# Hybrid encoder layer on one core: first modulation as matrix products, first loads reordered, and the first products of token half 0 placed ahead of the transposes of half 1

## Chip, core and metric

The kernel runs on one core of one Trainium2 chip. The metric is device time in microseconds (us) of one execution, the median of several runs. Engines are named as the profile names them: PE is TensorE (its weight loads are PEld), DVE is VectorE, ACT is ScalarE, POOL is GpSimd, SP is SyncE, whose queue here issues nearly all transfers.

## What is computed

One encoder layer over 1024 tokens of width 1024, all in float32. A conditioning vector gives shift and scale; the normalised, modulated input `h` goes through one wide projection `u = h @ w_in`, whose column groups feed four mixers.

```
cond = silu(c)
mod = cond @ mod_w + mod_b            # sh1, sc1, g1, sh2, sc2, g2
h = rms_norm(x) * (1 + sc1) + sh1
u = h @ w_in
y = concat(ssd(u), attention(u), mlstm(u), hyena(u)) @ w_out
x = x + g1 * y
h = rms_norm(x) * (1 + sc2) + sh2
x = x + g2 * ((silu(h @ w_gate) * (h @ w_up)) @ w_down)
out = rms_norm(x)
```

The Hyena mixer needs long filters that depend on weights alone: a small MLP of sines (`hyena_mlp`), a third product, a decay and a norm, then a 2048-point transform in two steps, sixteen-point sums on DVE and a table product on PE (`hyena_filters`). "First modulation" below is `sh1` and `sc1`, 2048 columns of `cond @ mod_w`.

## The kernel before

`build` (L286) runs the layer in one program. A scheduler reads the recorded operations and writes one fixed order of instructions for each engine; every engine then works through its own list in that order and waits where an operand is not ready. Tiles come from pools with a given number of buffers; a buffer that is taken again waits for its last reader.

The opening is `hyena_mlp` (L691), then `start` (L398) with `hyena_filters` (L717) interleaved, then the rest of `hyena_filters`, then `hyena` (L819).

- `start` loads the first modulation matrix as 16 pieces of 512 KB (`mw`, L416), four for each quarter q of the columns. For q of 0, 1 and 2 DVE multiplies each [128, 512] block by one column of `cond` and adds it to `acc` (L420, L422; eight blocks for each q); for q = 3 ACT multiplies (L425) and POOL adds (L427). PE transposes the four sums (L447), DVE reduces them over the 128 rows (L449) and adds the bias (L451, L452): `mod1`.
- The eight tiles `x` of 128 tokens are loaded (L435), ACT squares and sums them (L437), `norm` scales them (L442). For each token half h and each 128 columns k, PE transposes four blocks into one PSUM tile (L460, tile `tps`), ACT applies scale and shift (L462, `tm`), and `K.split` writes a high part (L235, `hhi`) and a low part (L239, `hlo`), the low part on POOL for even k and on DVE for odd k.
- Between the second and the third quarter of the modulation, `start` calls the first stage of `hyena_filters` (order 0): for each of eight blocks a product `fps` (L736), `hf` (L741), its square on ACT (L744), sums on DVE (L745, L749, L750) and a product with ones (L746).
- Between half 0 and half 1 it loads and splits the first weight group (`w_group`, L469).
- `hyena` then runs six columns groups of the projection: `gemm_t` (L483) is 24 products for each half of the tokens (three products of high and low parts for each of eight k, line L493), and `conv3` (L509) takes both halves out of PSUM.
- After the filters come the two convolutions (`hyena_conv`, L775). Their first product is L790 (`fps<-yk,tab`) and the first DVE operation on it is L798 (`ta<-fps,ks`).

PSUM is held in two pools of four tiles: `pg` for `tps`, `gps` and `nps`, `pm` for the rest.

Of the kernel before, what the change touches and what calls it, by code (L numbers as in the profile page):

```python
# [285 lines left out]
def build(nc, tc, d, out, dbg=None, dump=None):  # L286
    K = Net(nc, tc, d, out)
    with ExitStack() as es:
# [56 lines left out]
        with ExitStack() as e2:  # L345
            K.pm = psum("pm", right, m=4)
            hp = pool("ht", e2)
            K.so = Tags(pool("so", e2), st=3)
            with ExitStack() as e3:
                fl = Tags(rpool("fl", e3), n4=2, n2=8, yk=3, n1=2, tab=3, ks=3)  # L350
                hyena_mlp(K, fl)
                K.wp = Tags(pool("wp", e2), raw=3, whi=2, wlo=2)
                with ExitStack() as e4:
                    hf = hyena_filters(K, fl)
                    w0 = []
                    start(K, hp, Tags(pool("st", e4), tm=2), lambda: next(hf), lambda: w0.extend(w_group(K, G_HY + 2, first=False)))
                for _ in hf:
                    pass
            mp = Tags(rpool("m2", right), mxw=2)
            m2 = modulation2(K, mp)  # L360
            with ExitStack() as e3:
                hyena(K, Tags(rpool("hy", e3), n4=2, n2=8, yk=9, tab=3, tai=3, ks=2, rt=2), w0)
# [12 lines left out]
            mlstm(K, Tags(rpool("ml", right), va=2))  # L375
            project_na(K)
# [18 lines left out]
            _dump(K, dump)  # L395


def start(K, hp, sp, between, mid):  # L398

    nc, d = K.nc, K.d  # L400
    V = nc.vector

    accs, mts = {}, {}
    slots = [f"{t}{k}" for k in range(NK) for t in ("hhi", "hlo")]
    for qs in ((0, 3), (1,), (2,)):
        if qs == (2,):
            between()
        for q in qs:
            accs[q] = sp.tile([P, 512], F32, f"acc{q}")
        for k in range(NK):  # L410
            for q in qs:

                acc, c = accs[q], K.cond[:, k:k + 1]
                if k % 2 == 0:
                    mts[q] = hp.tile([P, 2, 512], F32, name="mw", tag=slots.pop(0))
                    nc.sync.dma_start(mts[q], d["modw1"][q, :, k:k + 2].rearrange("p k s c -> p k (s c)"))  # L416
                w = mts[q][:, k % 2]
                if q < 3:
                    if k == 0:
                        V.tensor_scalar_mul(acc, w, c)  # L420
                    else:
                        V.scalar_tensor_tensor(acc, in0=w, scalar=c, in1=acc, op0=ALU.mult, op1=ALU.add)  # L422
                else:
                    t = acc if k == 0 else sp.tile([P, 512], F32, "pr", bufs=2)
                    nc.scalar.activation(t, w, AF.Identity, scale=c)  # L425
                    if k > 0:
                        nc.gpsimd.tensor_tensor(acc, acc, t, op=ALU.add)  # L427
    ss = sp.tile([P, 8], F32, "ss")
    xs = []
    for g in range(4):  # L430
        xt = K.wp.tile([P, NK, 288], F32, ("whi", "wlo")[g % 2], name="x").rearrange("p a b -> p (a b)")
        for i in range(2):
            x = xt[:, i * D:(i + 1) * D]
            n = 2 * g + i
            nc.sync.dma_start(x, d["x"][n * P:(n + 1) * P, :])  # L435
            jk = K.so.tile([P, D], F32, "st", name="jk")
            nc.scalar.activation(jk, x, AF.Square, accum_out=ss[:, n:n + 1])  # L437
            xs.append(x)
# [5 lines left out]
    for q in (0, 3, 1, 2):  # L444
        ps = K.pm.tile([P, 512], F32, tag="m", name="psm")
        for n in range(4):
            nc.tensor.transpose(ps[:, n * P:(n + 1) * P], accs[q][:, n * P:(n + 1) * P], K.ident)  # L447
        mc = sp.tile([P, 2, 2], F32, "mc", bufs=2)
        V.tensor_reduce(mc, ps.rearrange("p (s k x) -> p s k x", s=2, k=2), axis=AX.X, op=ALU.add)  # L449
        mv = K.mod1.rearrange("p (s k) -> p s k", s=2)[:, :, 2 * q:2 * q + 2]  # L450
        V.tensor_tensor(mv, mc, K.pc[:, PC_MODB:PC_MODB + 16].rearrange("p (s k) -> p s k", s=2)[:, :, 2 * q:2 * q + 2], op=ALU.add)  # L451
        V.tensor_scalar_add(mv[:, 1], mv[:, 1], 1.0)  # L452
    K.hhi = [hp.tile([P, L], F32R, name=f"hhi{k}", tag=f"hhi{k}") for k in range(NK)]
    K.hlo = [hp.tile([P, L], F32R, name=f"hlo{k}", tag=f"hlo{k}") for k in range(NK)]
    for h in range(2):
        norm(h)
        for k in range(NK):
            ps = K.pg.tile([P, 512], F32, tag="g", name="tps")
            for i in range(4):
                nc.tensor.transpose(ps[:, i * P:(i + 1) * P], xs[h * 4 + i][:, k * P:(k + 1) * P], K.ident)  # L460
            t = sp.tile([P, 512], F32, tag="tm") if k % 2 else K.so.tile([P, 512], F32, "st", name="tm")
            nc.scalar.activation(t, ps, AF.Identity, bias=K.mod1[:, k:k + 1], scale=K.mod1[:, 8 + k:9 + k])  # L462
            c = slice(h * 512, (h + 1) * 512)
            K.split(K.hhi[k][:, c], K.hlo[k][:, c], t, "dve", "dve" if k % 2 else "pool")
        if h == 0:
            mid()


def w_group(K, n, gate=False, first=True):  # L469
# [10 lines left out]
    return whi, wlo  # L480


def gemm_t(K, whi, wlo, j):  # L483

    nc = K.nc
    c = slice(j * P, (j + 1) * P)
    pss = []
    for h in range(2):
        t = slice(h * 512, (h + 1) * 512)
        ps = K.pg.tile([P, 512], F32, tag="g", name="gps")  # L490
        seq = [(w, x, k) for k in range(NK) for w, x in ((whi, K.hhi), (whi, K.hlo), (wlo, K.hhi))]
        for n, (w, x, k) in enumerate(seq):
            nc.tensor.matmul(ps, lhsT=w[:, k, c], rhs=x[k][:, t], start=n == 0, stop=n == len(seq) - 1)  # L493
        pss.append(ps)
    return pss


def gemm_n(K, whi, wlo, i, N=256):
# [1287 lines left out]
```

## Time and profile before

| | |
|---|---|
| median of 3 runs | 1533.58 us (1527.52 to 1534.27) |
| the profiled execution | 1531.33 us, span 1529.5 us |
| PE busy | 1412.3 us, 92% of the span |
| DVE busy | 1043.3 us, 68% |
| ACT busy | 527.6 us, 34% |
| POOL busy | 91.4 us, 6% |
| mean granted TensorE clock | 0.974 of 2.4 GHz |
| HBM read and written | 195.17 and 60.59 MB |

Busy time is the time in which an engine had an instruction under way. The page cuts the span into 40 slices of 38.2 us; PE reads 2, 5, 8, 9 tenths in the first four, and 8 or 9 in nearly all later ones. DVE reads 7, 9, 9, 8, 9 in the first five. In the chain of work that ended last PE has 74% of the span, DVE 13%, DMA 5%.

### The profile page before, as it was taken

Reading aid. Unit: us, or ns where it says so; the run is one execution under the profiler, and the core shown is the slowest. Engines: PE = TensorE matmul, PEld = TensorE weight load, DVE = VectorE, ACT = ScalarE, POOL = GpSimd, SP = SyncE. Lnnn points to the kernel's source line nnn. Section 1 sums busy time; section 2 is a strip of 40 time slices with the busy share of each in tenths; the row PEclk is TensorE's granted clock in tenths of the full one; section 3 lists DMA queues with packets and bytes.
Section 4 is the critical chain, followed back from the end, with each engine's and each line's share of the span. In section 5 each row is a group of like instructions: output and inputs, shape, how many; then the busy total and the mean of one; then the engine's idle time right before and its main releaser. Section 6 shows DMA issues by size and latency. Waiting matters only on the chain.

```text
span 1529.5 us, 19231 instructions
## 1 busy us (share of the span) xinstructions
PE 1412.3 (92%) x6849; PEld 1141.0 (75%) x6849; DVE 1043.3 (68%) x2004; ACT 527.6 (34%) x958; POOL 91.4 (6%) x143
## 2 busy tenths in 40 slices
PE   2589979998998998989989999999999999999997
PEld 0366768876797777867767777888888888888886
DVE  7998977977847684687865476477777766335327
ACT  2522221232242342333456775322222223224222
POOL 2110000000102231230000000000000000000000
PEclk9789999999998999999999999999999999999999
DMA  6534467577653325476426457554444448643402
GB/s 247 194 104 143 128 197 230 185 225 226 190 185 110 105 87 155 125 265 203 154 87 217 150 170 276 201 180 164 148 144 153 149 164 305 222 149 123 153 1 110
DMA packets 134899, 257.02 MB, mean 168 GB/s; under 512 B 24703, under 2 KB 69663, under 8 KB 134804
## 3 DMA queue, kind: packets, MB, share of 16 engines
q1 hardware_dynamic: 111508, 228.50, 45.4%
q10 hardware_dynamic: 22688, 25.99, 4.8%
q0 software_dynamic: 608, 1.31, 0.3%
q8 instruction: 54, 0.88, 0.2%
q14 instruction: 41, 0.34, 0.1%
HBM read 195.17 MB, written 60.59 MB: 167 GB/s over the span
## 4 chain that ended last, share of the span: by engine, by line
PE 74%; DVE 13%; DMA 5%; issue 2%; ACT 2%; POOL 2%; SPq 0%; DVEq 0%; ACTq 0%; POOLq 0%
PE dps L1742 14%; PE X L1603 12%; PE gps L493 9%; PE Z L1603 8%; PE Y L1603 8%; PE gps L505 4%; PE gps L1554 3%; PE nS L1427 2%; PE ops L1554 1%; DMA mxw<-modw 1%; PE nS L1405 1%; DVE wlo L239 1%; PE kps L763 1%; PE mpa L1339 1%; DVE acc L422 1%
## 5 line engine op out<-in xcount | busy, mean ns | idle before, releaser
L1742 PE MATMUL dps<-wdh,ah 128*128 128x512 f32 x352 | 136.9, 389 | 0.0
L1742 PE MATMUL dps<-wdh,al 128*128 128x512 f32 x352 | 136.9, 389 | 0.0
L1742 PE MATMUL dps<-wdl,ah 128*128 128x512 f32 x352 | 136.9, 389 | 0.0
L493 PE MATMUL gps<-hhi,whi 128*128 128x512 f32 x320 | 130.7, 408 | 3.8 <-ACT nt L529 3.8
L493 PE MATMUL gps<-hlo,whi 128*128 128x512 f32 x320 | 129.6, 405 | 0.0
L493 PE MATMUL gps<-hhi,wlo 128*128 128x512 f32 x320 | 129.0, 403 | 0.0
L1603 PE MATMUL Z<-hp,wgh 128*128 128x512 f32 x352 | 95.4, 402 | 1.9 <-ACT ps L1658 1.6
L239 DVE TENSOR_TENSOR al<-ar,ah 128x1024 fp32r<-128x1024 f32 x44 | 53.4, 1222 | 47.9 <-ACT ah L233 47.9
L505 PE MATMUL gps<-whi,hhi 128*128 128x256 f32 (+1 forms) x256 | 77.5, 303 | 1.5 <-ACT z L529 1.5
L1603 PEld LDWEIGHTS Z<-hp,wgh 128*128 128x128 f32 x352 | 63.7, 188 | 19.8 <-ACT ps L1658 5.3
L505 PE MATMUL gps<-whi,hlo 128*128 128x256 f32 (+1 forms) x256 | 77.2, 302 | 0.0
L505 PE MATMUL gps<-wlo,hhi 128*128 128x256 f32 (+1 forms) x256 | 77.1, 301 | 0.0
L1742 PEld LDWEIGHTS dps<-wdl,ah 128*128 128x128 f32 x352 | 66.1, 188 | 13.8
L1742 PEld LDWEIGHTS dps<-wdh,al 128*128 128x128 f32 x352 | 66.1, 188 | 13.7
L1742 PEld LDWEIGHTS dps<-wdh,ah 128*128 128x128 f32 x352 | 66.1, 188 | 13.6
L493 PEld LDWEIGHTS gps<-hhi,whi 128*128 128x128 f32 x320 | 60.6, 189 | 19.5 <-ACT nt L529 5.0
L493 PEld LDWEIGHTS gps<-hhi,wlo 128*128 128x128 f32 x320 | 60.5, 189 | 13.8 <-issue 1.6
L233 ACT CAST ah<-ar 128x1024 fp32r<-128x1024 f32 x44 | 45.7, 1048 | 72.5 <-PE dps L1742 42.7
L493 PEld LDWEIGHTS gps<-hlo,whi 128*128 128x128 f32 x320 | 60.6, 189 | 12.4 <-issue 0.8
L1603 PE MATMUL X<-A,t4s 128*128 128x512 f32 x264 | 63.4, 389 | 0.0
L239 DVE TENSOR_TENSOR wdl<-wdr,wdh 128x1024 fp32r<-128x1024 f32 x22 | 26.9, 1224 | 53.1 <-ACT wdh L233 53.1
L1498 DVE SCALAR_TENSOR_TENSOR mxacc<-mxw,cond,mxacc 128x512 f32<-128x512 f32 x56 | 42.0, 750 | 29.2 <-DMA mxw<-modw 28.9
(500 smaller groups left out, 3240.5 us busy)
## 6 DMA issues: line engine op xcount, KB each, us to landing
wg<-wg SPq DMA_DIRECT2D x44, 512.0 KB
ar<-ad SPq DMA_DIRECT2D x44, 512.0 KB
mxw<-modw SPq DMA_DIRECT2D x64, 256.0 KB
raw<-w_in SPq DMA_DIRECT2D x28, 512.0 KB
psd<-ps SPq DMA_DIRECT2D x22, 512.0 KB
psr<-psd SPq DMA_DIRECT2D x22, 512.0 KB
wu<-wu SPq DMA_DIRECT2D x22, 512.0 KB
wdr<-wd SPq DMA_DIRECT2D x22, 512.0 KB
```

Source lines behind the costliest of these rows:

```text
L233: nc.scalar.copy(hi, src)
L239: e.tensor_tensor(lo, src, hi.bitcast(F32), op=ALU.subtract)
L422: V.scalar_tensor_tensor(acc, in0=w, scalar=c, in1=acc, op0=ALU.mult, op1=ALU.add)
L493: nc.tensor.matmul(ps, lhsT=w[:, k, c], rhs=x[k][:, t], start=n == 0, stop=n == len(seq) - 1)
L505: nc.tensor.matmul(ps, lhsT=x[k][:, t], rhs=w[:, k, :N], start=n == 0, stop=n == len(seq) - 1)
L763: nc.tensor.matmul(ps, lhsT=tab[:, la], rhs=y[:, 0], start=True, stop=not cx)
L1339: nc.tensor.matmul(pa[:, 2 * j + dr], lhsT=sds[dr][:, h], rhs=va[:, h], start=True, stop=True)
L1427: nc.tensor.matmul(pb[:, 448:512], lhsT=pT[:w * 40, n], rhs=vw[:w * 40, n, c:c + 64], start=n == 0, stop=n == len(chunks) - 1)
L1498: V.scalar_tensor_tensor(acc, in0=mt, scalar=K.cond[:, k:k + 1], in1=acc, op0=ALU.mult, op1=ALU.add)
L1554: K.nc.tensor.matmul(ps, lhsT=l, rhs=r, start=n == 0, stop=n == 5)
L1603: nc.tensor.matmul(ps, lhsT=w[a][:, k], rhs=x[k][b], start=start and n == 0, stop=n == 11, skip_group_check=not start)
L1742: nc.tensor.matmul(acc[i], lhsT=x[:, ts], rhs=m, start=f == 0 and n == 0, stop=f == NF - 1 and n == 2)
```

## The change

`start` becomes a generator that `build` drives in stages. The stages, in the order in which they are recorded: loads and squares of `x` tiles 0 to 3; `hyena_mlp`; loads of the modulation's quarter 0; load and split of the first weight group; loads of quarters 1 to 3 and of `x` tiles 4 to 7, then for each quarter its modulation and the two columns k of half 0 that need it; the products of the first weight group with half 0, both j (`gemm_half`); the columns of half 1; the products with half 1; and only then the first stage of `hyena_filters`.

The modulation of a quarter is eight float32 products on PE with one column of `cond` as the stationary operand (1 x 512 out), a copy of that row by ACT, four products that turn the row into four columns, and two small DVE operations. The sums on DVE, ACT and POOL and the reduction are gone. `x` tiles 0 to 3 have tiles of their own; the extra pool tag `tm` is gone, and all `tm` tiles come from the three `st` buffers.

```
+                    st = start(K, hp, Tags(pool("st", e4)))
+                    next(st)
+                    hyena_mlp(K, fl)
+                    next(st)
+                    w0 = w_group(K, G_HY + 2, first=False)
+                    next(st)
+                    pss = [[gemm_half(K, *w0, j, 0)] for j in range(2)]
+                    for _ in st:
+                        pass
+                    for j in range(2):
+                        pss[j].append(gemm_half(K, *w0, j, 1))
+                    next(hf)
...
+    for n in range(4):
+        load_x(n, sp.tile([P, D], F32, f"x{n}"))
+    yield
...
+    def load_w(q):
+        for k in range(0, NK, 2):
+            t = hp.tile([P, 2, 512], F32, name="mw", tag=f"{('hhi', 'hlo')[k // 2 % 2]}{2 * q + k // 4}")
+            nc.sync.dma_start(t, d["modw1"][q, :, k:k + 2].rearrange("p k s c -> p k (s c)"))
+            mts.append(t)
+
+    def modulation(q):
+
+        ps = K.pm.tile([P, 512], F32, tag="m", name="mps")[0:1]
+        for k in range(NK):
+            nc.tensor.matmul(ps, lhsT=K.cond[:, k:k + 1], rhs=mts[4 * q + k // 2][:, k % 2], start=k == 0, stop=k == NK - 1)
+        row = K.so.tile([1, 512], F32, "st", name="row")
+        nc.scalar.copy(row, ps)
+        mc = K.pm.tile([P, 512], F32, tag="m", name="mcs")[:, :4]
+        for i in range(4):
+            nc.tensor.matmul(mc[:, i:i + 1], lhsT=row[:, i * P:(i + 1) * P], rhs=K.ones[0:1, 0:1], start=True, stop=True)
...
+    load_w(0)
+    yield
+    for q in (1, 2, 3):
+        load_w(q)
+    xt = [K.wp.tile([P, NK, 288], F32, t, name="x").rearrange("p a b -> p (a b)") for t in ("whi", "wlo")]
+    for n in range(4):
+        load_x(4 + n, xt[n // 2][:, n % 2 * D:(n % 2 + 1) * D])
+    norm(0)
+    K.hhi, K.hlo = [], []
+    for q in range(4):
+        modulation(q)
+        for k in (2 * q, 2 * q + 1):
+            columns(0, k)
+    yield
+    norm(1)
+    for k in range(NK):
+        columns(1, k)
...
+def gemm_half(K, whi, wlo, j, h):
+
+    c = slice(j * P, (j + 1) * P)
+    t = slice(h * 512, (h + 1) * 512)
+    ps = K.pg.tile([P, 512], F32, tag="g", name="gps")
+    seq = [(w, x, k) for k in range(NK) for w, x in ((whi, K.hhi), (whi, K.hlo), (wlo, K.hhi))]
+    for n, (w, x, k) in enumerate(seq):
+        K.nc.tensor.matmul(ps, lhsT=w[:, k, c], rhs=x[k][:, t], start=n == 0, stop=n == len(seq) - 1)
+    return ps
```

`hyena` takes the two finished pairs of PSUM tiles instead of the weights. Lines after `start` move by 15: L736 becomes L751, L790 becomes L805, L798 becomes L813; the products L493 are L504, the transposes L460 are L458, L437 is L417.

What the scheduler makes of it shows at three places.

PE, where the first modulation ends and the transposes begin, before (`psm` are the transposes of the modulation's sums, `tps` those of `x`, `kps` table products of the filters, `gps` the first projection products):

```order
L447 MATMUL psm<-ident,acc_406 128x128 x4
L460 MATMUL tps<-ident,x 128x128 x48
L763 MATMUL kps<-yk,tab 128x256 x2
L460 MATMUL tps<-ident,x 128x128 x8
L763 MATMUL kps<-yk,tab 128x256
L460 MATMUL tps<-ident,x 128x128 x8
L765 MATMUL kps<-yk,tab 128x256
L493 MATMUL gps<-hhi_488,whi_590 128x512
```

and of the change, from the second product of the sine MLP to the third quarter of the modulation (`mps` is the row of a quarter, `mcs` its four columns, `x_200` to `x_212` the `x` tiles 0 to 3):

```order
L727 MATMUL fps<-h_226,w_220 64x512 x2
L436 MATMUL mps<-mw,cond 1x512 x8
L441 MATMUL mcs<-ones,row 128x1 x4
L436 MATMUL mps<-mw,cond 1x512 x8
L458 MATMUL tps<-ident,x_200 128x128
L458 MATMUL tps<-ident,x_204 128x128
L458 MATMUL tps<-ident,x_208 128x128
L458 MATMUL tps<-ident,x_212 128x128
L458 MATMUL tps<-ident,x_200 128x128
L458 MATMUL tps<-ident,x_204 128x128
L441 MATMUL mcs<-ones,row 128x1 x4
L436 MATMUL mps<-mw,cond 1x512 x8
```

The four quarters now stand on PE one behind the other, each behind the row copy of the quarter ahead of it, and the last two quarters and the 48 products of half 0 stand ahead of half 1.

ACT, of the change, around the copy of the first row (`h_237` is the output of the sine MLP, `jk,ss<-x` the squares of `x` tiles 4 to 7):

```order
L703 ACTIVATE h_237<-su 128x512
L417 ACTIVATE jk,ss<-x 128x1024 x4
L438 COPY row<-mps 1x512
L249 ACT_TABLE_LOAD
L249 ACTIVATE ln1t<-ln1v 128x4
L460 ACTIVATE tm<-tps,mod_66 128x512 x2
L438 COPY row<-mps 1x512
L460 ACTIVATE tm<-tps,mod_66 128x512 x2
```

The first row copy stands behind the squares of the last four `x` tiles, the last of the large loads of the opening.

DVE, before, from the end of the sine MLP into the filter loop (`acc_286`, `acc_406` are sums of the modulation, `hf`, `s`, `hp` and `hm` the filter loop):

```order
L687 TENSOR_SCALAR su<-su 128x512
L422 SCALAR_TENSOR_TENSOR acc_286<-mw,cond,acc_286 128x512 x5
L741 TENSOR_TENSOR hf<-fps,dc 128x512
L420 TENSOR_SCALAR acc_406<-mw,cond 128x512
L422 SCALAR_TENSOR_TENSOR acc_406<-mw,cond,acc_406 128x512
L745 TENSOR_TENSOR s_317<-s_317 128x256
L749 TENSOR_TENSOR hp<-hf 128x256
```

and of the change, from the last quarter's `mod` to the first filter operation:

```order
L443 TENSOR_TENSOR mod_66<-mcs,pc 128x2x2
L445 TENSOR_SCALAR mod_66<-mod_66 128x2
L235 CAST hhi_463<-tm 128x512
L235 CAST hhi_474<-tm 128x512
L239 TENSOR_TENSOR hlo_475<-tm,hhi_474 128x512
L235 CAST hhi_343<-tm 128x512
L756 TENSOR_TENSOR hf<-fps,dc 128x512
L235 CAST hhi_354<-tm 128x512
L239 TENSOR_TENSOR hlo_355<-tm,hhi_354 128x512
```

The filter loop has moved from ahead of the first `hhi` to behind the first `hhi` of half 1 (the second `hhi_343`, one and the same tile for both halves).

## Rows read from the trace of the kernel before

**Rows 1.** The page: busy time of each engine, share of the span, instructions.

```profile
PE 1412.3 (92%) x6849; PEld 1141.0 (75%) x6849; DVE 1043.3 (68%) x2004; ACT 527.6 (34%) x958; POOL 91.4 (6%) x143
```

**Rows 2.** Busy time by stretch: length, PE, PEld, DVE, ACT, POOL, clock, DMA share, GB/s.

```profile
82.25:219.52 137.27, 124.65 (x556) 96.97 (x555) 122.99 (x247) 39.71 (x60) 6.05 (x5) 0.96 0.43 134
0.00:82.25 82.25, 33.13 (x106) 17.02 (x107) 71.61 (x129) 33.02 (x54) 16.99 (x17) 0.84 0.64 218
```

**Rows 3.** Timeline of DVE: start, duration, line; first `hhi` of half 1, first convolution operation.

```profile
82.25 0.43 DVE L235 CAST hhi<-tm 128x512 fp32r<-128x512 f32 x1 [0.36 <-ACT tm L462]
...
219.52 0.69 DVE L798 TENSOR_TENSOR ta<-fps,ks 128x512 f32<-128x512 f32 x1 [1.22 <-PE fps L793]
```

**Rows 4.** Waits of DVE between 82.25 and 219.52: us in total, times, longest.

```profile
DVE ks L767 <- PE kps L765: 5.5, 6, 1.9
DVE n L551 <- ACT z L529: 2.5, 1, 2.5
```

**Rows 5.** Waits of PE between 86.04 and 219.52, same columns.

```profile
PE kps L763 <- DVE yk L591: 3.0, 1, 3.0
```

**Rows 6.** Groups of DVE by line, 0 to 82.25: busy, mean ns, idle before.

```profile
L422 DVE SCALAR_TENSOR_TENSOR acc<-mw,cond,acc 128x512 f32<-128x512 f32 x21 | 18.6, 885 | 0.4
...
L250 DVE RECIPROCAL fnr<-fnt 128x256 f32<-128x256 f32 x1 | 1.7, 1748 | 0.0
```

**Rows 7.** Timeline of DVE in the filter loop.

```profile
42.59 0.42 DVE L750 TENSOR_TENSOR hm<-hf 128x256 f32<-128x256 f32 x1
42.92 0.69 DVE L741 TENSOR_TENSOR hf<-fps,dc 128x512 f32<-128x512 f32 x1
43.52 0.42 DVE L745 TENSOR_TENSOR s<-s 128x256 f32<-128x256 f32 x1
```

**Rows 8.** Busy time of PE by stretch: length, PE, clock, DMA share, GB/s.

```profile
0.00:10.00 10.00, 1.97 (x4) 1.00 0.59 188
7.00:20.00 13.00, 2.42 (x6) 1.00 1.02 407
80.00:85.00 5.00, 4.99 (x23) 0.63 0.43 147
```

**Rows 9.** Timeline of SP's queue and ACT: first loads, a copy, a square, a `tm`.

```profile
2.12 0.43 SPq L695 DMA_DIRECT2D ft<-c_feats  x1
...
4.16 8.40 SPq L416 DMA_DIRECT2D mw<-modw  x12
...
19.95 1.18 ACT L713 COPY t<-fps 64x512 f32<-64x512 f32 x2 [0.83 <-PE fps L712]
...
40.90 1.06 ACT L437 ACTIVATE jk<-x 128x1024 f32<-128x1024 f32 x1 [0.76 <-DMA x<-x]
...
72.79 0.78 ACT L462 ACTIVATE tm<-tps,mod 128x512 f32<-128x512 f32 x1 [0.30 <-DVE hlo L239]
```

**Rows 10.** Timeline of PE: transposes after idle, first projection product, float32 products.

```profile
80.01 1.97 PE L460 MATMUL tps<-ident,x 128*128 128x128 f32 x8 [5.70 <-DVE x L442]
...
84.92 1.04 PE L460 MATMUL tps<-ident,x 128*128 128x128 f32 x8
...
86.04 0.58 PE L493 MATMUL gps<-hhi,whi 128*128 128x512 f32 x1
...
98.64 1.06 PE L765 MATMUL kps<-yk,tab 128*128 128x256 f32 x2
99.49 1.06 PE L763 MATMUL kps<-yk,tab 128*128 128x256 f32 x2
...
109.88 0.59 PE L763 MATMUL kps<-yk,tab 128*128 128x256 f32 x2
110.31 0.59 PE L765 MATMUL kps<-yk,tab 128*128 128x256 f32 x2
...
592.59 1.10 PE L1527 MATMUL mgp<-mxacc,ones 128*128 128x512 f32 x2 [0.81 <-DMA mxacc<-macc]
```

**Rows 11.** The chain that ended last, 100 to 112: start, us, what.

```profile
101.17 8.87 PE gps L493 x39
```

More of the change, by code (lines that the diff above doesn't have):

```diff
@@ L350, in build @@
                 fl = Tags(rpool("fl", e3), n4=2, n2=8, yk=3, n1=2, tab=3, ks=3)
-                hyena_mlp(K, fl)
                 K.wp = Tags(pool("wp", e2), raw=3, whi=2, wlo=2)
@@ L354, in build @@
                     hf = hyena_filters(K, fl)
-                    w0 = []
-                    start(K, hp, Tags(pool("st", e4), tm=2), lambda: next(hf), lambda: w0.extend(w_group(K, G_HY + 2, first=False)))
+                    st = start(K, hp, Tags(pool("st", e4)))
[10 more added lines that the diff above has]
+                    next(hf)
                 for _ in hf:
@@ L361, in build @@
             with ExitStack() as e3:
-                hyena(K, Tags(rpool("hy", e3), n4=2, n2=8, yk=9, tab=3, tai=3, ks=2, rt=2), w0)
+                hyena(K, Tags(rpool("hy", e3), n4=2, n2=8, yk=9, tab=3, tai=3, ks=2, rt=2), pss)
             project_ssd(K, lambda: next(m2, None))
@@ L395, in build, with start @@
             _dump(K, dump)
-def start(K, hp, sp, between, mid):
+def start(K, hp, sp):
     nc, d = K.nc, K.d
     V = nc.vector
[L403 to L427, printed above, removed]
@@ L428, in start, with load_x @@
     ss = sp.tile([P, 8], F32, "ss")
     xs = []
[L430 to L438, printed above, removed]
+    def load_x(n, x):
+        nc.sync.dma_start(x, d["x"][n * P:(n + 1) * P, :])
+        jk = K.so.tile([P, D], F32, "st", name="jk")
+        nc.scalar.activation(jk, x, AF.Square, accum_out=ss[:, n:n + 1])
+        xs.append(x)
@@ new lines, in start @@
+    for n in range(4):
+        load_x(n, sp.tile([P, D], F32, f"x{n}"))
+    yield
+    mts = []
+    def load_w(q):
[12 more added lines that the diff above has]
+            nc.tensor.matmul(mc[:, i:i + 1], lhsT=row[:, i * P:(i + 1) * P], rhs=K.ones[0:1, 0:1], start=True, stop=True)
+        mv = K.mod1.rearrange("p (s k) -> p s k", s=2)[:, :, 2 * q:2 * q + 2]
+        V.tensor_tensor(mv, mc.rearrange("p (s k) -> p s k", s=2),
+                        K.pc[:, PC_MODB:PC_MODB + 16].rearrange("p (s k) -> p s k", s=2)[:, :, 2 * q:2 * q + 2], op=ALU.add)
+        V.tensor_scalar_add(mv[:, 1], mv[:, 1], 1.0)
@@ L442, in norm @@
             V.tensor_scalar_mul(xs[4 * h + i], xs[4 * h + i], r[:, i:i + 1])
[L444 to L464, printed above, removed]
-        if h == 0:
-            mid()
+    def columns(h, k):
+        if h == 0:
+            K.hhi.append(hp.tile([P, L], F32R, name=f"hhi{k}", tag=f"hhi{k}"))
+            K.hlo.append(hp.tile([P, L], F32R, name=f"hlo{k}", tag=f"hlo{k}"))
+        ps = K.pg.tile([P, 512], F32, tag="g", name="tps")
+        for i in range(4):
+            nc.tensor.transpose(ps[:, i * P:(i + 1) * P], xs[h * 4 + i][:, k * P:(k + 1) * P], K.ident)
+        t = K.so.tile([P, 512], F32, "st", name="tm")
+        nc.scalar.activation(t, ps, AF.Identity, bias=K.mod1[:, k:k + 1], scale=K.mod1[:, 8 + k:9 + k])
+        c = slice(h * 512, (h + 1) * 512)
+        K.split(K.hhi[k][:, c], K.hlo[k][:, c], t, "dve", "dve" if k % 2 else "pool")
@@ L480, in w_group @@
     return whi, wlo
-def gemm_t(K, whi, wlo, j):
[L485 to L495, printed above, removed]
+def gemm_half(K, whi, wlo, j, h):
[6 more added lines that the diff above has]
+    return ps
+def gemm_t(K, whi, wlo, j):
+    return [gemm_half(K, whi, wlo, j, h) for h in range(2)]
 def gemm_n(K, whi, wlo, i, N=256):
@@ L816, in hyena_conv, with hyena @@
     dft16_inv(K, sp, g, Z)
-def hyena(K, sp, w0):
+def hyena(K, sp, pss0):
     nc = K.nc
@@ L824, in hyena @@
     for n in (1, 2, 0):
-        whi, wlo = w0 if n == 1 else w_group(K, G_HY + 2 * n)
+        w = n != 1 and w_group(K, G_HY + 2 * n)
         for j in range(2):
-            pss = gemm_t(K, whi, wlo, j)
+            pss = gemm_t(K, *w, j) if w else pss0[j]
             acc = K.so.tile([P, L], F32, "st", name="acc")
```

## Prediction

> **What bounds the kernel now.** I read the page first: PE is busy for 92% of the span, DVE for 68% [rows 1]. That is a mean over stages, so I looked for the point up to which the change reorders anything. Counting the instructions of both orders gives it: ahead of the first convolution product (`fps<-yk,tab`, L790) both kernels have done the same 288 projection products of line 493, the same 64 table products of the filters and the same 38 products of line 505, and DVE's list is the same again from its first operation on that product (`ta`, L798). I call this the common point; it stands at 219.52 us [rows 3]. Behind it both lists agree, so a delay there should be a delay of the whole kernel.
>
> Next I read busy time up to that point, cut at the first `hhi` of half 1 (82.25), which both kernels contain. From there to the common point DVE is busy 122.99 of 137.27 us and PE 124.65 [rows 2]. Both look full. The waits tell them apart: late in that stretch PE stands idle 3.0 us for a `yk` of the filters, a DVE result [rows 5], while DVE waits 5.5 us for products in six pieces and 2.5 once for ACT [rows 4]. So up to the common point the chain is DVE's list, with short trips through PE; PE is close behind. Ahead of 82.25 DVE is busy 71.61 of 82.25 us and PE only 33.13 [rows 2]. The opening is therefore DVE's, and the question is how much of DVE's work the new opening leaves for later.
>
> **What is removed.** 24 multiply-adds on DVE (21 take 18.6 us [rows 6]; the three first ones and the four reductions add some 4): about 22 us, and ACT's and POOL's quarter. This is the gain the change could have. It counts only if DVE does other work in that time.
>
> **The new opening, in order of time.**
>
> Loads. In the first 10 us 188 GB/s flow, 1.88 MB; saturated it is 407 GB/s [rows 8]. The first large load is now issued where `ft` was, at 2.12 and not at 4.16 [rows 9], so I count 1.88 MB at 8.0. Up to the last `x` tile 26 pieces of 0.524 MB and 0.31 MB of small ones must land: (13.94 - 1.88) / 0.407 = 29.6 us, so at 37.6.
>
> First row copy. Quarter 0 on PE is done by then, but the copy of its row stands on ACT behind the squares of `x` tiles 4 to 7, and each square takes 1.06 and a short read-out of its sum [rows 9]. The last ends near 38.9. The copy has one partition and 512 columns; the nearest row is 0.59 for 64 partitions [rows 9]. With four tiny products behind it quarter 1 starts on PE at 40.1.
>
> Quarters 1 to 3. No row shows a product with one column out. The price is that of the columns that stream: a float32 product over 256 columns follows the next after 0.43 at 2.4 GHz (109.88, 110.31) and after 0.85 at 1.2 GHz (98.64, 99.49) [rows 10], so over 512 it is 0.86 or 1.71. A quarter of eight is 6.9 at 2.4 GHz and 13.7 at 1.2. Alone, with other work between, one took 1.05 [rows 10], 8.4 for a quarter. Below nothing it can't cost, since PE has nothing else to do there. PE has idled before quarter 1. In the 5 us from 80, behind an idle stretch, the granted clock is 0.63 on average [rows 8], that is 3.7 us at 1.2 GHz and then 2.4, and eight transposes went from 1.97 at 80.01 to 1.04 at 84.92 [rows 10]. So quarter 1: 3.5 us at half speed for two products, six at 0.86, done at 48.8. Row copy and columns, partly under six transposes: 1.1. Quarter 2 done at 56.8, quarter 3 at 64.8, four transposes 0.5: the first products at 65.3, against 86.04 now [rows 10].
>
> Products of half 0. 48 at 8.87 / 39 = 0.227 [rows 11], 10.9 and 0.3 for the last columns: done at 76.5. The transposes of half 1 stand behind them. One group (0.5) and one `tm` (0.78 [rows 9]): DVE writes the first `hhi` of half 1 at 78.0. That is 4.2 us earlier than the 82.25 of now.
>
> DVE up to there. Scaling, two sine layers, two `wlo` and half 0 are some 22 us; DVE idles the other 56. The filter loop that filled this time stands behind the first `hhi` of half 1 in its list, so it can't start.
>
> DVE behind it. To the 122.99 us that it does today come eight rounds of the loop. From the starts, `hf` takes 0.60 and each of three others 0.33 [rows 7]: 8 x 1.59 = 12.7. Then the head of the transform that today lies ahead of 82.25: two operations over 1024 columns (1.2 each by the same pace), three over 512 or with a table (0.6), seven of 256 (0.33) and the reciprocal, 1.75 [rows 6]: 8.3 with the small ones, less what two finish under each other, 7.5. Together 20.2. So 143.2 us of DVE work. POOL's four low parts of half 1 run beside DVE in both kernels, so what they hold up is in the 123 already.
>
> Idle of DVE on the way: 14.28 now (137.27 - 122.99 [rows 2]). With PE now ahead of DVE, waits for queued products shrink, the dependent ends stay. Bounds 4 and 14; I take 8, since about half of the waits [rows 4] are such ends.
>
> **Sum.** 78.0 + 143.2 + 8 = 229.2 for the common point, against 219.5: **9.7 us later**. Against the profiled execution (1531.33) 1541.0; its time lies 2.25 under the median of the runs, 1533.58, so **1543.3** there. The lower end: quarters at full clock throughout (-2) and idle of 4 gives +4. The upper: 1.05 a product (+4.5) and idle of 14 gives +20. Other edits: the lost `tm` tag leaves three `st` buffers, hidden while DVE is the later engine; the 512 KB loads that leave the queue's later part are off the path; two free PSUM tiles of `pg` in the transposes of half 1 (two hold the products of half 0) slow them to ACT's 0.78 a column, still under DVE's pace of 1.2 or more.
>
> **Rivals.**
>
> *The clock stays at 1.2 GHz through the four quarters.* Quarters 1 to 3 then take 41.1 us and not 22.5, and the first 3.5 us of products run at half speed too: 18.6 + 1.8 = 20.4 more, so +30 (22 to 40), 1564. For it: a product with one column out is unlike anything in the trace. Against it: transposes, float32 table products and 64-row products all had the full clock once the work was dense. The Trainium skill ("TensorE: Matmul & The Clock Gate", section "What's actually happening") says that activity releases the throttle, and names no kind of product; for every kind that the trace holds it agrees. The same page ("Part 4: PE-mode transpose") says that transposes do not count as busy in the same way, by which kinds do differ; there the trace disagrees, since the transposes at 84.92 ran at full speed [rows 10].
>
> *Faster: PE sets the common point, not DVE.* PE reaches its first products 20.7 us earlier. Left over for later are 32 transposes (0.13 each [rows 10], 4.2), eight `fps` and eight sums (1.05 and 0.6 at most, halved where two `fps` run side by side: 9) and a few table products (2.2), 15.4, so PE is 5.3 us ahead; with the wait for `yk` [rows 5] gone as well, it is -8.3, about 1525. It decides whether DVE can write its last `yk` some 20 us sooner than I count, that is, whether the half 1 `hhi` comes at 60 and not at 78. The order speaks against it.
>
> *Absorbed: the delay is real at the common point and lost later*, because the convolutions wait for something that doesn't move. Price +0 to +4, 1535. Against it: every transfer of that stage is issued behind instructions that move with it.
>
> **How the numbers follow.** Forecast 0.55, half clock 0.25, absorbed 0.12, faster 0.08. A measurement of this kernel tells about 0.5% from no change, 7.7 us. Forecast at +4 to +20: a third of it lies under 7.7. So slower 0.25 + 0.37 + a little = 0.64, same 0.12 + 0.18 - a little = 0.28, faster 0.08. The range takes in the forecast's own +4 to +20, most of absorbed and all but the top of the half clock: 1533 to 1566; the forecast's own is 1537 to 1554.
>
> **What would show it.** Right: first products near 65; the first `hhi` of half 1 near 78; DVE idle for over 40 us before it; `ta` near 229; PE with many short waits for DVE from 90 to 220, where it now has few; behind `ta` the two traces run in step. The row copies' first one starts where the last square ends. Wrong: quarters of 13 us (half clock); `ta` at or ahead of 219 with DVE still full (DVE idles less than I think, or PE leads); a difference that grows or shrinks behind `ta`.

## Result and profile after

The changed kernel takes 1550.28 us (median of four runs, 1546.91 to 1554.95); the kernel before, run beside it, 1533.92. The ratio is 1.011 with a 95% interval of 1.0062 to 1.0159: **slower**, by 1.1%. The profiled executions are 17.2 us apart (1548.56 and 1531.33).

The busy row of the page and busy time by stretch, cut at the first `hhi` of half 1 and at the first `ta` (columns as in [rows 2]):

```profile
PE 1440.0 (93%) x6929; PEld 1143.7 (74%) x6929; DVE 1022.1 (66%) x1976; ACT 529.2 (34%) x956; POOL 79.5 (5%) x136
```

```profile
0.00:84.39 84.39, 60.00 (x194) 25.40 (x194) 28.90 (x57) 28.17 (x43) 5.50 (x9) 0.94 0.52 197
84.39:239.30 154.91, 126.73 (x548) 93.67 (x547) 142.79 (x292) 44.97 (x69) 6.07 (x6) 0.94 0.41 127
239.30:1546.70 1307.40, 1253.30 (x6191) 1024.60 (x6189) 850.42 (x1629) 456.08 (x845) 67.93 (x121) 0.99 0.51 169
```

DVE does 21 us less over the whole program (1043.3 before [rows 1]), PE 28 us more. Up to `ta` DVE's saving is 22.9 us: 28.90 + 142.79 = 171.7 against 71.61 + 122.99 = 194.6 [rows 2]. Yet `ta` comes 19.8 us later, since DVE's idle time ahead of the first `hhi` of half 1 went from 10.6 us to 84.39 - 28.90 = 55.5. Behind `ta` 1307.4 us remain, against 1529.5 - 219.52 = 1310.0 before: the delay is carried to the end, less 2.6 us.

The timeline of DVE at the two cuts (answers to [rows 3]), and DVE's waits between them (answers to [rows 4]):

```profile
84.39 0.43 DVE L235 CAST hhi<-tm 128x512 fp32r<-128x512 f32 x1 [8.04 <-ACT tm L460]
...
239.29 0.69 DVE L813 TENSOR_TENSOR ta<-fps,ks 128x512 f32<-128x512 f32 x1 [1.22 <-PE fps L808]
```

```profile
DVE ks L782 <- PE kps L780: 3.2, 7, 1.1
DVE n L566 <- ACT z L544: 2.5, 1, 2.5
DVE ks L782 <- DMA kspec<-ks: 2.2, 4, 1.0
DVE ta L813 <- PE fps L808: 1.2, 1, 1.2
```

The opening on ACT (the last square, the row copies of quarters 0 and 1) and on PE (the quarters, the first product, the last product of half 0, the first transposes of half 1):

```profile
39.45 1.06 ACT L417 ACTIVATE jk<-x 128x1024 f32<-128x1024 f32 x1 [0.64 <-DMA x<-x]
40.42 0.19 ACT L417 ACTIVATION_READ_ACCUMULATOR jk<-x 128x1 f32 x1
40.63 0.57 ACT L438 COPY row<-mps 1x512 f32<-1x512 f32 x1
...
52.98 0.57 ACT L438 COPY row<-mps 1x512 f32<-1x512 f32 x1 [7.85 <-PE mps L436]
```

```profile
24.23 8.98 PE L436 MATMUL mps<-mw,cond 128*1 128x512 f32 x16
41.35 1.83 PE L441 MATMUL mcs<-ones,row 1*128 1x1 f32 x8 [8.13 <-ACT row L438]
43.11 9.78 PE L436 MATMUL mps<-mw,cond 128*1 128x512 f32 x16
...
54.60 7.03 PE L436 MATMUL mps<-mw,cond 128*1 128x512 f32 x16
...
63.34 7.03 PE L436 MATMUL mps<-mw,cond 128*1 128x512 f32 x16
...
70.71 0.48 PE L504 MATMUL gps<-hhi,whi 128*128 128x512 f32 x1
71.12 1.05 PE L441 MATMUL mcs<-ones,row 1*128 1x1 f32 x8
...
82.65 0.39 PE L504 MATMUL gps<-hhi,wlo 128*128 128x512 f32 x1
82.88 1.03 PE L458 MATMUL tps<-ident,x 128*128 128x128 f32 x8
```

Quarter 0 is done at 33.2, and PE then waits 8.13 us for a row copy that stands behind four squares on ACT. From 43 to the last transposes of half 1 PE works without a gap, but what it works on is the modulation, and DVE waits for it. In the second stretch PE waits for DVE, longest of all for the last `yk` (at 208.9 and 226.0 us):

```profile
PE kps L778 <- DVE yk L606: 10.0, 2, 5.9
PE kps L778 <- DVE yk L563: 3.8, 3, 1.8
```

### The profile page after: what moved, and what is told of

Its sections match the earlier page's. It is cut to its first block, busy times and chain, and to the rows that moved or that the text cites. A ratio compares the mean times of both kernels' runs of the same rounds, so it can differ in the third digit from the quotient of the medians.

```text
span 1546.7 us, 19356 instructions
## 1 busy us (share of the span) xinstructions
PE 1440.0 (93%) x6929; PEld 1143.7 (74%) x6929; DVE 1022.1 (66%) x1976; ACT 529.2 (34%) x956; POOL 79.5 (5%) x136
## 3 DMA queue, kind: packets, MB, share of 16 engines
q1 hardware_dynamic: 111508, 228.50, 44.9%
## 4 chain that ended last, share of the span: by engine, by line
PE 75%; DVE 10%; DMA 7%; issue 3%; ACT 2%; POOL 2%; SPq 0%; POOLq 0%; DVEq 0%; ACTq 0%
PE dps L1757 14%; PE X L1618 12%; PE gps L504 10%; PE Z L1618 8%; PE Y L1618 8%; PE gps L520 3%; PE gps L1569 3%; PE nS L1442 2%; PE mps L436 2%; PE ops L1569 1%; PE nS L1420 1%; DMA mxw<-modw 1%; DMA x<-x 1%; PE mpa L1354 1%; DMA mkv<-mvk 1%
## 5 line engine op out<-in xcount | busy, mean ns | idle before, releaser
L504 PE MATMUL gps<-hhi,whi 128*128 128x512 f32 x320 | 130.9, 409 | 3.8 <-ACT nt L544 3.8
L504 PE MATMUL gps<-hhi,wlo 128*128 128x512 f32 x320 | 129.3, 404 | 0.0
L504 PE MATMUL gps<-hlo,whi 128*128 128x512 f32 x320 | 129.1, 403 | 0.0
L1757 PEld LDWEIGHTS dps<-wdh,al 128*128 128x128 f32 x352 | 66.1, 188 | 13.8
L504 PEld LDWEIGHTS gps<-hhi,whi 128*128 128x128 f32 x320 | 60.7, 190 | 19.6 <-ACT nt L544 4.9
L504 PEld LDWEIGHTS gps<-hhi,wlo 128*128 128x128 f32 x320 | 60.7, 190 | 13.9 <-issue 1.6
L504 PEld LDWEIGHTS gps<-hlo,whi 128*128 128x128 f32 x320 | 60.6, 189 | 12.4 <-issue 0.8
```

Source lines behind the costliest of these rows:

```text
L504: K.nc.tensor.matmul(ps, lhsT=w[:, k, c], rhs=x[k][:, t], start=n == 0, stop=n == len(seq) - 1)
L1757: nc.tensor.matmul(acc[i], lhsT=x[:, ts], rhs=m, start=f == 0 and n == 0, stop=f == NF - 1 and n == 2)
```

## Experiments

My theory going in: `ta` = first `hhi` of half 1 + DVE's work behind it + 12 to 16 us of waits. Rival: PE's work up to `ta` sets it. The table has all runs; its times are read from one profiled execution of each kernel. That the three terms add up to `ta` is so in any kernel; what the theory adds is that the waits stay between 12 and 16 us. "Idle ahead" is DVE's idle time before the first `hhi` of half 1. The ratio is that of all runs to the kernel before on the same chip; medians of different runs come from several chips, on which the kernel before took 1529.3 to 1533.9, so they are compared by their ratios.

| kernel | first `hhi` of half 1 | idle ahead | DVE work behind | waits behind | `ta` | ratio to before |
|---|---|---|---|---|---|---|
| before | 82.25 | 10.6 | 123.0 | 14.3 | 219.5 | 1 |
| changed | 84.39 | 55.5 | 142.8 | 12.1 | 239.3 | 1.0110 (1.0062 to 1.0159) |
| e1 loop between quarters | 101.58 | 50.8 | 120.6 | 15.4 | 237.5 | 1.0099 (1.0060 to 1.0139) |
| e2 half 1 first | 74.34 | 46.2 | 145.1 | 26.7 | 246.2 | 1.0142 (1.0100 to 1.0184) |
| e3 both | 88.80 | 48.9 | 130.9 | 23.0 | 242.7 | 1.0132 (1.0082 to 1.0183) |
| e4 squares late | 74.05 | 44.2 | 142.8 | 16.2 | 233.0 | 1.0084 (1.0049 to 1.0118) |
| e9 short quarters | 70.64 | 42.3 | 142.9 | 14.8 | 228.3 | 1.0062 (1.0038 to 1.0085) |
| e5 loop mid | 86.96 | 42.0 | 127.7 | 17.2 | 231.9 | 1.0064 (1.0040 to 1.0089) |
| e7 dense quarters | 83.58 | 40.3 | 129.3 | 14.9 | 227.8 | 1.0061 (1.0034 to 1.0087) |
| e8 quarter 0 first | 84.28 | 40.8 | 129.4 | 16.0 | 229.7 | 1.0065 (1.0048 to 1.0083) |
| e10 two quarters on PE | 82.29 | 17.7 | 119.8 | 13.3 | 215.4 | 0.9968 (0.9946 to 0.9990) |
| e11 all on PE | 88.18 | 33.5 | 117.8 | 13.3 | 219.3 | 1.0037 (1.0017 to 1.0058) |
| e14 half 0 ahead | 91.97 | 13.6 | 116.1 | 11.2 | 219.3 | 1.0016 (1.0000 to 1.0031) |
| e15 seven `dc` buffers | 85.03 | 16.7 | 116.9 | 16.7 | 218.6 | 0.9992 (0.9973 to 1.0011) |

The waits leave that range by more than 1.5 us in two rows, e2 and e3: there half 1 stands ahead of the products of half 0, and the rival was the better account.

### e1: the filter loop between the quarters (changed kernel)

```
-                    next(hf)
...
         modulation(q)
         for k in (2 * q, 2 * q + 1):
             columns(0, k)
+        filt()
...
-        if o == 0:
-            yield
+            if o == 0 and j in (4, 5, 6, 7):
+                yield
```

> Undoes one part of the change: the eight rounds of the filter loop are recorded two by two behind the four quarters of the modulation, not behind half 1. Theory (up to the common point the time is DVE's list, and the change left its opening idle and put 20.2 us of the filters behind the first hhi of half 1): DVE does the loop before that hhi, which itself moves by under 4 us; ta comes 12 to 20 us earlier than in the changed kernel (239.3), at 219 to 227, and the time falls by as much, to 1530 to 1538. Rival (PE's work up to the common point sets it): ta within 4 us of 239 and the time within 4 us of 1550. Second rival (squares and products of the loop between the quarters hold up ACT's row copies and PE): the first products come 5 us or more later than 70.7 and eat half of the gain or more.

Measured: median 1545.09; `ta` at 237.5. The second rival was right: the first products came at 83.33 and not at 70.71. DVE's work behind half 1 fell by 22 us, and the first `hhi` of half 1 came 17 us later. The timeline of PE, one quarter:

```profile
60.07 1.13 PE L751 MATMUL fps<-w,h 64*128 64x512 f32 x4
61.13 2.73 PE L435 MATMUL mps<-mw,cond 128*1 128x512 f32 x6
64.98 0.70 PE L761 MATMUL nps<-s,ones 128*128 128x256 f32 x2 [1.12 <-DVE s L760]
65.61 1.88 PE L435 MATMUL mps<-mw,cond 128*1 128x512 f32 x4
67.42 0.70 PE L761 MATMUL nps<-s,ones 128*128 128x256 f32 x2
68.04 2.74 PE L435 MATMUL mps<-mw,cond 128*1 128x512 f32 x6
...
72.50 1.13 PE L751 MATMUL fps<-w,h 64*128 64x512 f32 x4
```

The loop's products (1.06 and twice 0.63 by the starts) and one wait of 1.12 for a sum go into PE's series. A quarter's step is 12.4 us (72.50 - 60.07 from one `fps` to the next), not 8.74 (63.34 - 54.60). In an opening that PE sets, the loop is not free.

### e2 and e3: half 1 ahead of the products of half 0

```
-                    pss = [[gemm_half(K, *w0, j, 0)] for j in range(2)]
                     for _ in st:
                         pass
-                    for j in range(2):
-                        pss[j].append(gemm_half(K, *w0, j, 1))
+                    pss = [gemm_t(K, *w0, j) for j in range(2)]
```

e3 is e1 and e2 together.

> Undoes another part: both halves are transposed before any product of the first weight group; the loop stays behind half 1. Theory (DVE's list starts with the first hhi of half 1): that hhi no longer waits for the 48 products of half 0 and comes 11 to 12 us earlier, near 73; DVE's work behind it stays 143 us, so ta at 227 to 232 and the time 8 to 12 us shorter, 1538 to 1542. Rival (PE sets the common point): PE gives up 12 us of early products and waits for DVE's splits of half 1, so ta is the same or up to 6 us later, 1550 to 1556.

> Both edits together: loop between the quarters, and half 1 transposed ahead of the products of half 0. Theory: hhi of half 1 near 73 and 123 us of DVE work behind it with 8 to 14 us of waits would put ta at 204 to 212; PE, whose products of half 0 now come later, may then be the later one, so ta at 207 to 220 and 1520 to 1532; less than the sum of the two gains. Rival (PE sets the common point): no shorter than with the loop moved alone.

Measured: medians 1551.54 and 1550.67. In e2 the first `hhi` of half 1 came 10 us earlier, near where the theory had it, and `ta` 6.9 us later, by the rival's sign and a little beyond its 6. e3's `ta` is 5.2 us behind e1's: the rival there too. The waits of e2 say how; of DVE behind that `hhi`, and of ACT from it to 140 us:

```profile
DVE ks L780 <- PE kps L778: 9.2, 14, 1.3
DVE wlo L239 <- ACT whi L233: 8.3, 2, 8.1
...
ACT whi L233 <- PE gps L502: 9.6, 2, 5.2
```

PE starts the first products at 79.7, ACT stands with `acc` behind them, the next group's `whi` behind `acc`, and DVE's `wlo` behind that. So in this order the 48 early products, which hold the first `hhi` of half 1 back by 10 us, were worth more at `ta` than those 10 us. In the kernel before the same move (e14 below) is worth nothing.

### e4: squares of tiles 4 to 7 behind the row copies

```
         nc.sync.dma_start(x, d["x"][n * P:(n + 1) * P, :])
-        jk = K.so.tile([P, D], F32, "st", name="jk")
-        nc.scalar.activation(jk, x, AF.Square, accum_out=ss[:, n:n + 1])
         xs.append(x)
...
+    for n in range(4, 8):
+        square(n)
     yield
     norm(1)
```

> The squares of x tiles 4 to 7 are recorded behind the four quarters, so that the first row copy does not stand behind them on ACT. Nothing else moves. Theory (the opening is a chain, and the first row copy waits for a load that is not its own): quarter 1 starts near 35.6 and not at 43.1, the first products, the first hhi of half 1 and ta all come 6 to 8 us earlier, and the time is 1542 to 1544. Rival (the quarters wait for their matrix pieces, which land as late as the x tiles, or the squares only move the wait to half 1): first hhi of half 1 and time within 2 us of the changed kernel's 84.4 and 1550.

Measured: 1544.56, `ta` at 233.0 (6.3 us earlier). The first row copy on ACT and quarter 1 on PE:

```profile
32.07 0.57 ACT L442 COPY row<-mps 1x512 f32<-1x512 f32 x1 [1.82 <-PE mps L440]
```

```profile
33.74 7.03 PE L440 MATMUL mps<-mw,cond 128*1 128x512 f32 x16
```

Quarter 1 starts 9.4 us earlier than in the changed kernel and takes 7.03 us instead of 9.78: PE idles 0.8 us ahead of the columns and not 8.1, and the granted clock is 1.00 from 33.7 to 40.8 here, where it was 0.50 from 40 to 45 in the changed kernel. So the first products come 12.1 us earlier (58.60), 10.3 us of it arrive at the first `hhi` of half 1, and 4.1 of those are lost again to more waiting behind it.

### e9: the price of the quarters' products

```
-        for k in range(NK):
+        ks = range(NK) if q == 0 else (1, 7)
+        for k in ks:
```

> Prices the modulation on PE: quarters 1 to 3 keep two of their eight products (18 float32 products over 512 columns are left out, so most of the modulation of these quarters is missing); order, loads and everything else as in the changed kernel. Theory (the opening is PE's quarters in series, 7.03 us each, with row copy and columns between): first products 15 to 16 us earlier, near 55; first hhi of half 1 near 69 (84.4 now); ta 11 to 16 us earlier, 223 to 228; time 1534 to 1539. Rival (loads or ACT's row copies hold the opening): first products less than 8 us earlier, time over 1543.

Measured: 1537.99, first `hhi` of half 1 at 70.64, `ta` at 228.3. The 18 products at 0.88 (7.03 / 8) are 15.8 us; 14.3 arrive at the first products (56.38), 13.8 at that `hhi`, 11.0 at `ta`. By the ratios the gain is 0.5%, some 7 us, and their intervals overlap. This is the largest single piece of the loss that the runs show, 11.0 of the 19.8 us at `ta`.

### e5, e7, e8: what the opening gains without PE's gaps

All have the late squares of e4. e5 records the loop ahead of the products of half 0; e7 adds the next quarter's products ahead of this quarter's row copy; e8 adds the loads and products of quarter 0 ahead of `hyena_mlp`.

```
+                    next(hf)
                     pss = [[gemm_half(K, *w0, j, 0)] for j in range(2)]
...
+    products(0)
     for q in range(4):
+        if q < 3:
+            products(q + 1)
         modulation(q)
```

> On top of late squares (ta 233.0, first hhi of half 1 at 74.05, time 1544.6) the filter loop is recorded between the columns of half 0 and the products of half 0, so that it needs no PE between the quarters. Theory (the loop between quarters gained 19 us of DVE behind half 1 and lost 17 ahead of it, because PE waited for its sums): now DVE does the loop while PE does the products of half 0; first hhi of half 1 at 74 to 84, DVE's work behind it 123 to 130 us and not 143, ta at 214 to 226, time 1526 to 1537. Rival (PE has become the later engine up to the common point): ta at 229 or later and time over 1540.

> As the one before, and the eight products of the next quarter are recorded ahead of the row copy and columns of this one, so that PE has no gap between quarters (three gaps of 1.7 us in the changed kernel). Theory: first products 4 to 5 us earlier than with the loop alone, ta 2 to 5 us earlier, time 1522 to 1534. Rival (the matrix pieces land no sooner than PE asks for them): no difference.

> As the one before, and the loads and products of quarter 0 are recorded ahead of the sine MLP, so that PE does not hold them behind the MLP's product L727 (which starts at 22.3 in the changed kernel, quarter 0 at 24.2). Theory (the four quarters in series on PE set the opening, from the time the first one starts): quarter 0 starts at 12 to 16, first products near 50, ta 4 to 9 us earlier than without, 206 to 218, time 1517 to 1528, under before's 1530. Rival (quarter 3 waits for its pieces, which land near 34, or the clock is low that early, so each product takes twice as long): first products and time within 3 us of the kernel without this edit.

Measured: 1539.61, 1539.75 and 1539.35; `ta` at 231.9, 227.8 and 229.7. All three lie above the range the theory gave, by 3, 6 and 11 us. e7's `ta` came 4.1 us earlier than e5's as expected, but its first products only 1.2 us earlier (57.14, 4 to 5 expected), and the median gained nothing. The loop left DVE's stretch behind half 1 (15 us less than e4), but it now lies with the products of half 0 ahead of half 1, whose first `hhi` came 13 us later. In e8 quarter 0 began at 12.1, but quarter 1 still ended at 39.1 (38.6 in e7):

```profile
12.10 8.95 PE L440 MATMUL mps<-mw,cond 128*1 128x512 f32 x16 [12.10 <-DMA mw<-modw]
20.98 1.08 PE L733 MATMUL fps<-ft,w 33*64 33x512 f32 x4
...
29.20 1.97 PE L741 MATMUL fps<-h,w 64*64 64x512 f32 x4 [5.25 <-ACT h L717]
31.10 7.99 PE L440 MATMUL mps<-mw,cond 128*1 128x512 f32 x16
```

Quarter 1 stands behind the sine MLP's second product in PE's list and waits for it as before; and the MLP's first product now stands behind quarter 0, at 20.98 (11.68 in e7), so that its second one comes 7 us later than in e7 (29.20, 22.05). DVE's idle time ahead of half 1 stays near 41 us in all three: in this order DVE has little to do while PE does the modulation.

### e10, e11: the modulation on PE in the order before

From the kernel before; loads, loop and halves stay as they are. e10 moves quarters 1 and 2, e11 all four.

```
+                if q in ON_PE:
+                    nc.tensor.matmul(acc, lhsT=c, rhs=w, start=k == 0, stop=k == NK - 1)
+                    if k == NK - 1:
+                        columns(q, acc)
-                if q < 3:
+                elif q < 3:
```

> The kernel before, with quarters 1 and 2 of the modulation on PE (eight products, row copy by ACT, four column products) and quarters 0 and 3 on DVE, ACT and POOL as before; loads, filter loop and order of the halves as before. Theory (ta comes 123 us of DVE work and 12 to 16 us of waits behind the first hhi of half 1, wherever that stands; before, DVE is full up to it and PE idle): 11 to 13 us of DVE sums go, PE's 14 us of products lie in its idle time, the first hhi of half 1 comes at 69 to 74 (82.25), ta at 206 to 213 (219.5), time 1517 to 1525 against before's 1530. Rival (PE in its own order has to wait for the loop's sums between the products, as when the loop stood between the quarters, or the last x tile holds the opening): that hhi at 80 or later, time within 4 us of before.

> The kernel before, with all four quarters on PE and nothing else of the change: loads, filter loop and order of the halves as before. Theory (the modulation on PE is a gain as long as the loop fills DVE beside it; what lost in the changed kernel is the order around it): 22 us of DVE work go from the opening, first hhi of half 1 at 64 to 76, ta at 201 to 215, time 1512 to 1527. Rival (four quarters in series on PE with the loop's products between them set the opening, whatever else): first hhi of half 1 at 82 or later, time 1530 or more.

Measured: e10 1524.70, which is **faster than both kernels** (by 0.3% against before, 1529.32 beside it), at the slow end of the theory's range; e11 1535.85, the rival. In both the first `hhi` of half 1 stood where the rival had it, and e10's `ta` lies behind the theory's 213: its time is in the range, its mechanism is not the theory's. e10's gain is 4.2 us at `ta` where 10 us of DVE work went (184.4 up to `ta`, 194.6 before); by the table it comes from 3.2 us less work and 1.0 less waiting behind that `hhi`, not from an earlier `hhi`. In e11 22 us of work went and 23 us of idle time came. The profiled execution of e11 (1530.87) is among its shorter ones, that of e10 (1530.18) among its longer ones, so e11's row in the table looks better than its median and e10's looks worse. The timeline of ACT in e11 (row copy of the last quarter, first and last square):

```profile
53.88 0.57 ACT L410 COPY row<-mps 1x512 f32<-1x512 f32 x1 [1.81 <-PE mps L439]
...
54.89 1.04 ACT L461 ACTIVATE jk<-x 128x1024 f32<-128x1024 f32 x1
...
62.16 1.04 ACT L461 ACTIVATE jk<-x 128x1024 f32<-128x1024 f32 x1
```

### e14: only the products of half 0 ahead

```
+                    def mid():
+                        w0.extend(w_group(K, G_HY + 2, first=False))
+                        pss.extend([gemm_half(K, *w0, j, 0)] for j in range(2))
```

> The kernel before, with only the 48 products of half 0 placed ahead of the transposes of half 1. Theory (in the changed kernel PE was the later engine without this, so it gained 7 us at ta there; in the kernel before DVE's list sets ta): the first hhi of half 1 moves from 82.25 to 84 to 93, DVE fills part of that with its next transform work, ta unchanged or up to 6 us later, time 1530 to 1536. Rival (it helps PE here as well): ta 4 to 8 us earlier, time 1522 to 1526.

Measured: 1531.50, `ta` at 219.3, the first `hhi` of half 1 9.7 us later: DVE did transform work in that time (78.4 us ahead of it, 71.6 before). As the theory had it, and a part of the change that by itself costs at most 0.3%.

### e15: e10 with seven buffers for `dc`

```
-fl = Tags(rpool("fl", e3), n4=2, n2=8, yk=3, n1=2, tab=3, ks=3)
+fl = Tags(rpool("fl", e3), n4=2, n2=8, yk=3, n1=7, tab=3, ks=3)
```

> The kernel with quarters 1 and 2 on PE, and seven buffers in place of two for the tiles dc of the filter loop. The loads of x stand behind those of dc in SP's list, and each dc load waits until the loop has read an older one: before and with two quarters on PE the x tiles were issued one by one from 34 to 46 us, with 145 GB/s from 30 to 40. Theory (that wait of SP, not DVE, held the first hhi when DVE had less to do, so that hhi stayed at 69 and the first of half 1 at 82): x tiles issued by 30, landed by 42, first hhi of half 1 at 72 to 78, ta at 205 to 212 (215.4), time 1514 to 1521 against before's 1529. Rival (PE's mixed list of loop and quarters sets the opening): x tiles earlier, but half 1 at 80 or later and the time within 3 us of 1524.7.

Measured: 1530.16, `ta` at 218.6. The theory fell, and half 1 stands where the rival had it, but the time is 5.5 us above e10's median (0.24% by the ratios, whose intervals overlap), outside the rival's 3 us too. By the table the first `hhi` of half 1 came 2.7 us later than in e10 and DVE waited 3.4 us more behind it; why stays open. SP issued all eight tiles in one go, where e10 issued four of them one by one from 34.15 and was done at 46.2; and ACT did not look at them until its row copy was done (SP's queue; ACT's row copy, first and last square):

```profile
34.30 6.10 SPq L459 DMA_DIRECT2D x<-x  x8
...
53.62 0.57 ACT L410 COPY row<-mps 1x512 f32<-1x512 f32 x1 [1.67 <-PE mps L439]
54.11 1.05 ACT L461 ACTIVATE jk<-x 128x1024 f32<-128x1024 f32 x1
...
61.39 1.04 ACT L461 ACTIVATE jk<-x 128x1024 f32<-128x1024 f32 x1
```

In the changed kernel the row copy waits behind squares whose tiles come late; here eight squares wait behind a row copy whose quarter comes late (in e10 at 50.47). Both are one list of ACT with the later item in front. That a kernel with squares ahead of the last row copy would turn e10's remaining idle time into a gain was read from these rows and not tried.

## Why the prediction was right, and what it missed

The sign, the mechanism and the range held; the size was 1.011, where 1543.3 / 1533.58 = 1.0063 was named. On the profiled executions I had 9.7 us and 17.2 came, near the upper end of the forecast's own +4 to +20. By my own steps:

- **The common point and what lies behind it** held. In all fourteen kernels `ta` lies between 215.4 and 246.2, and 1303.8 to 1313.0 us remain behind it: 1310.2 on average in the five with `ta` under 220, 1306.9 in the nine above 227. So most of a delay at `ta` stays, and a few us of it may come back (single executions); "absorbed later" fell as the account of this change.
- **Last `x` tile, first row copy**: the copy does start where the last square ends, at 40.63 instead of 38.9, and with its columns (1.83 at the low clock, where I had allowed 1.2 for both) quarter 1 began 3.0 us late.
- **Quarters**: 9.78 and twice 7.03 measured, 8.7 and twice 6.9 predicted. The price of a one-column product, taken from the columns that stream, was right. (The upper bound of 1.05 a product misread [rows 10], whose line says 1.10; by it the upper end lies some 1 us higher.) Quarter 1's slow part was too short in my sum: low clock for 3.5 us, where the rows below give it until 48.7 (0.63 on average from 45 to 50), that is 5.6 us of the quarter, and 9.78 - 7.03 = 2.75 us of loss where I had 1.8. The gaps were 1.71 and not 1.1. First products 70.7, not 65.3.
- **Products of half 0** took 12.3 us instead of 11.2, since quarter 3's column products (1.05) stand among them. The first `hhi` of half 1: 84.39, not 78.0. That is 6.4 of the 7.5 us that the sum missed: a chain of steps of which nearly all were a little longer than costed.
- **DVE behind it**: 142.8 us measured, 143.2 predicted. Idle of DVE: 12.1, where I took 8 between bounds of 4 and 14. That term was mis-sized by 4.1: I had PE's lead shorten the waits by 6; they went from 14.3 to 12.1, those for `kps` from 5.5 [rows 4] to 3.2. Behind `ta` 2.6 came back: 6.4 - 0.4 + 4.1 - 2.6 = 7.5, which is what was missing.
- **Many short waits of PE for DVE**: came. From 90 to 220 PE waits for DVE nine times, 15.2 us in all; before it was four times and 8.7 us.
- **Half clock**: fell. The granted clock is 0.50 from 40 to 45 and 1.00 from 50 on, and products with one column out run at 7.03 a quarter. Busy time of the changed kernel by stretch (columns as in [rows 2]):

```profile
24.20:29.00 4.80, 4.80 (x9) 0.77 (x8) 4.63 (x8) 1.16 (x2) 0.00 (x0) 1.00 1.02 418
29.00:33.30 4.30, 4.21 (x10) 0.67 (x8) 0.63 (x2) 0.63 (x1) 0.00 (x0) 1.00 1.03 423
40.00:45.00 5.00, 3.65 (x11) 2.12 (x12) 1.58 (x9) 3.99 (x7) 0.00 (x0) 0.50 1.09 363
45.00:50.00 5.00, 5.00 (x8) 0.76 (x7) 4.77 (x6) 0.13 (x1) 1.26 (x1) 0.63 0.16 66
50.00:55.00 5.00, 5.00 (x22) 2.11 (x21) 0.25 (x2) 0.57 (x1) 0.00 (x0) 1.00 0.00 0
```

The Trainium skill ("TensorE: Matmul & The Clock Gate", section "What's actually happening") says that activity releases the throttle; for this kind of product the trace agrees.
- **"Faster: PE sets the common point"** fell as to the sign, but e2 shows how near it was: without the early products PE is the later engine. My sum charged those products with holding half 1 back and gave them no credit; the sum for the whole change came out with the right sign all the same, but of the part alone (e2 against changed, +6.9 at `ta`) it gives the wrong one.

What the change costs, part by part, as far as the runs show it at `ta`, in one execution each: the modulation in series on PE (e9, 11.0 us), the row copy behind late squares (e4, 6.3). The loop's place alone is worth 1.8 (e1), because moving it back into the opening loads PE. The half 0 products are worth keeping in this order. The parts overlap, so they don't add up. No variant of the changed kernel's order has a ratio under 1, and one column of the table goes with that: DVE's idle time ahead of half 1 never fell below 40 us there, where 10.6 + 22.9 = 33.5 would have used up the whole saving (e11 has just that, and its `ta` is that of before).

## What to carry over

Work that is taken off a full engine is a gain only as far as that engine has other work ready in that time: here 22.9 us of DVE work went and 44.9 us of idle time came, while half of the move (two quarters of four, with the old order) gained 0.3%. Write the end of a stage as start + work + waits of one engine, cut at instructions that every variant has, and check each variant against that sum: it says at once whether an edit shortened work, moved it ahead, or only turned it into waiting. And in a fixed list look for the late item in front of the ready ones, on every queue that the stage passes through, ACT and SP too; removing one such wait (e15, e8) gained nothing where the next list had one of its own.

## What was unexpected of the hardware

A float32 product with one column of `cond` as stationary operand, over 512 columns, stands in the trace as two instructions and costs 0.88 us at the full clock (7.03 / 8). That is twice the 0.43 at which products with 128 columns out and half as many streamed follow each other ([rows 10]): the one column saves nothing. Between 45 and 50 us the granted clock rose from 0.50 to 1.00 while PE did nothing but such products. Four tiny products (one row in, one column streamed; eight instructions) still took 1.05 us at the full clock and 1.83 at the low one.

The clock column of the changed kernel reads 1.00 in the first 38 us even where products run slowly: quarter 0 took 8.98 us at a stated 1.00, quarters 2 and 3 took 7.03. By the starts of quarter 0's instructions they followed each other every 0.85 us up to 28.2 us and every 0.43 behind it, and the trace's first record of the clock stands at 28.2. So ahead of its first record the column says nothing, and the pace of equal products is the better witness.

SP works through its list in order with its waits: in the kernel before the first four `x` tiles were issued one by one from 37.0 to 44.0, each behind a `dc` load, and the trace puts most of SP's waiting from 30 to 50 us down to DVE's `hf`, which reads `dc` (four times, 14.7 us). The Trainium skill ("DMA: Bandwidth & Descriptors", section "Anatomy of one DMA — SWDGE (gpsimd) path"), whose section is on loads issued by GpSimd, says that any semaphore wait happens on the issuing sequencer before dispatch; for SP's loads e15, where seven buffers let all eight tiles go within 6.1 us, agrees.
